# Two 32-byte tiles ahead of the products' operands

## The chip, the core and the metric

The kernel runs on one core of a Trainium2 chip. The core has a matrix engine (PE, with the loading of its stationary operand listed apart as PEld), a vector engine (DVE), a scalar engine (ACT), GpSimd (POOL) and a queue engine (SP) that starts the transfers. All engines share the on-chip memory SBUF, 128 partitions wide; the products are summed in PSUM. The metric is the device time of one execution in microseconds, lower being better.

## The reference

Two layers of a decoder over 512 tokens of width 1024. Each layer has two gated feed-forward blocks (FFN), a mixing block of three branches, and a gated input embedding; a norm stands before and after each.

```python
def swiglu(x, wg, wu, wd):
    return (jax.nn.silu(x @ wg) * (x @ wu)) @ wd
...
for i in range(DEPTH):
    f = swiglu(rmsnorm(h, g[0]), ffn_w_gate[i, 0], ffn_w_up[i, 0], ffn_w_down[i, 0])
    h = h + 0.5 * rmsnorm(f, g[1])
    z = rmsnorm(h, g[2]) @ w_in[i]
    ...                                   # spatial gating, RG-LRU, sparse attention -> y_a, y_b, y_c
    mix = jnp.concatenate([y_a, y_b, y_c], axis=-1) @ w_out[i]
    h = h + rmsnorm(mix, g[3])
    f = swiglu(rmsnorm(h, g[4]), ffn_w_gate[i, 1], ffn_w_up[i, 1], ffn_w_down[i, 1])
    h = h + 0.5 * rmsnorm(f, g[5])
    gate = jax.nn.sigmoid(rmsnorm(h, g[6]) @ ple_w_gate[i])
    h = h + rmsnorm(gate * (p[i] @ ple_w_proj[i]), g[7])
```

All of it is float32, and most of the work is in the products with the weights.

## The kernel before

The token axis lies along the free dimension: `h` is held as 8 blocks of 128 features by 512 tokens. Each float32 product is made of three products in the reduced type fp32r: both operands are split into a high part (rounded by ACT) and a low part (the rest, by DVE), and `mm3` (L271) adds high·high, high·low and low·high in one PSUM bank. In a name of the trace such as `mm<-xh,wh`, the first operand is the moving one (streamed, 256 or 512 columns) and the second the stationary one (loaded ahead, 128 columns).

Weights arrive as 4 KB per partition in a ring of eight `raw` tiles (L77, pool `p_raw`). ACT writes the high part into one of six `wh` tiles (L88) and DVE writes the low part into another `raw` tile; so `wh` is the high and `raw` the low stationary operand. Activations and everything else of 2 KB per partition lie in 56 slots tagged `big` and 7 tagged `scr` (L187): `xh`/`xl` (input of a block), `hh`/`hl` (hidden layer), `bh`/`bl` (combinations for the Strassen stage), `yh`/`yl` (branches' output), `zh`/`zl`.

An FFN runs as: 6 feature blocks of gate and up products; 16 more by Strassen's scheme (`strassen`, L725: seven products of 256 columns for each block, `bh`/`bl` moving, summed in `mm` and `o` banks); the down products (`hh`/`hl` moving, 512 columns; the last two blocks in halves of 256). The mixing block has the input projections, two stages in which the weights are the moving operand (`token_project`, L874: `wav` 256 columns and `wvg` 280 columns), the attention, and the `w_out` products (`yh`/`yl` moving). PE's order is written out by hand: each product depends on the one before it (L217).

Where a tile lies in SBUF is decided by the pools: `sb` lays one ring after another, in the order in which the tags are first asked for, each tile rounded up to a multiple of 32 bytes; `raw` follows behind it. `setup` (L278) asks for `ident`, `const`, `warm`, `h`, `cols`, and then come `big`, `scr`, `wh` and the small tags; `softplus` (L331) asks for some of the last small ones. So an odd number of 32-byte tiles ahead of a ring puts it at 32 bytes past a multiple of 64. In the built program:

| tile | first byte before | mod 64 | first byte after | mod 64 |
|---|---|---|---|---|
| `ident` | 16512 | 0 | 16512 | 0 |
| `h` | 17088 | 0 | 17120 | 32 |
| `cols` | 33472 | 0 | 33504 | 32 |
| `big` (first of 56) | 34144 | 32 | 34176 | 0 |
| `scr` (first of 7) | 148832 | 32 | 148864 | 0 |
| `wh` (first of 6) | 166304 | 32 | 166336 | 0 |
| `raw` (first of 8) | 196480 | 0 | 196544 | 0 |

The tiles of a ring are 1, 2 or 4 KB apart, so all of a ring have the same remainder. A `wvg` tile is the exception in use: it holds three pieces of 1120 bytes, so its middle piece lies 32 bytes off the other two.

Of the kernel before, what the change touches and what calls it, by code (L numbers as in the profile page):

```python
# [152 lines left out]
class Kern:  # L153
# [124 lines left out]
    def setup(self):  # L278
        nc, pool = self.nc, self.pool
        c = lambda name, shape: pool.tile(list(shape), F32, name=name)  # L280
        self.ident = c("ident", (128, 128))
        nc.gpsimd.memset(self.ident, 0.0)
        nc.gpsimd.affine_select(self.ident, self.ident, pattern=[[-1, 128]], compare_op=OP.not_equal,
                                fill=1.0, base=0, channel_multiplier=1)
        const = c("const", (128, 6))
        self.ones, self.mhalf, self.okrow = (const[:, i:j] for i, j in ((0, 1), (1, 2), (2, 6)))
        for t, value in ((self.ones, 1.0), (self.mhalf, -0.5), (self.okrow, 1.0)):
            nc.vector.memset(t, value)
        nc.gpsimd.affine_select(self.okrow[:, 0:1], self.okrow[:, 0:1], pattern=[[0, 1]],
                                compare_op=OP.is_ge, fill=0.0, base=-31, channel_multiplier=1)  # L290
        warm = self.small("warm", (128, 1), 1)
        nc.scalar.activation(warm, self.mhalf, AF.Silu)
        self.h = pool.tile([128, KD, S], F32, name="h")
        cols = c("cols", (128, L, 8 * KD + 20))
        nc.sync.dma_start(cols, self.dram["cols"])
        self.g = cols[:, :, :8 * KD].rearrange("p l (n k) -> p l n k", n=8)
        self.vec, at = {}, 8 * KD
        for name, n in (("conv_w", 8), ("conv_b", 2), ("ba", 2), ("bx", 2), ("lam", 2), ("cb1", 2), ("cb2", 2)):
            self.vec[name] = cols[:, :, at:at + n]
            at += n  # L300
        for n in (1, 5):
            nc.vector.tensor_scalar(self.g[:, :, n], self.g[:, :, n], 0.5, None, op0=OP.mult)
# [28 lines left out]
    def softplus(self):  # L331
        nc = self.nc
        lam = self.vec["lam"]
        sh = [128, L, 2]
        s = lambda n: self.small("sp" + n, sh, 1)
        e, u, u2, acc, m = s("e"), s("u"), s("v"), s("a"), s("m")
        self.pin("v", nc.vector.tensor_scalar(m, lam, -1.0, None, op0=OP.mult), False)
        nc.vector.tensor_max(e, m, lam)
        nc.scalar.activation(e, e, AF.Exp, scale=-1.0)
        nc.vector.tensor_scalar(u, e, 2.0, None, op0=OP.add)  # L340
        nc.vector.reciprocal(u, u)
        nc.vector.tensor_mul(u, u, e)
        nc.vector.tensor_mul(u2, u, u)
        terms = 9
        nc.vector.memset(acc, 1.0 / (2 * terms + 1))
        for i in range(terms - 1, -1, -1):
            nc.vector.tensor_mul(acc, acc, u2)
            nc.vector.tensor_scalar(acc, acc, 1.0 / (2 * i + 1), None, op0=OP.add)
        nc.vector.tensor_mul(acc, acc, u)
        nc.vector.tensor_scalar(m, m, 0.0, None, op0=OP.max)  # L350
        self.sp4 = self.small("sp4", sh, 1)
        nc.vector.scalar_tensor_tensor(self.sp4, acc, 2.0, m, op0=OP.mult, op1=OP.add)
        nc.vector.tensor_scalar(self.sp4, self.sp4, 4.0, None, op0=OP.mult)
        self.sp8 = self.small("sp8", sh, 1)
        nc.vector.tensor_scalar(self.sp8, self.sp4, -2.0, None, op0=OP.mult)
# [1104 lines left out]
```

## Time and profile before

| | |
|---|---|
| time, median of 3 runs | 2144.58 us (2143.4 to 2149.41) |
| the profiled execution | 2146.3 us, of which the span from first to last instruction is 2144.6 us |
| mean granted clock of PE | 0.993 of full speed |
| PE busy | 97% of the span, 14464 product records |
| PEld | 89% |
| DVE, ACT, POOL | 65%, 50%, 13% |
| HBM read | 192.78 MB, 92 GB/s over the span |

The page counts an engine as busy from the start of an instruction to its end, and products are pipelined: one is listed with 0.28 us while the next starts 0.12 us after it. So how fast PE goes is read from the starts of products that follow each other, not from their lengths. Where PE waits, the row says for whom.

### The profile page before, as it was taken

To read this page: it belongs to the slowest core of one execution; us is meant where nothing else is said; L and a number is where in the kernel's file an instruction comes from. 1 tells how busy PE (TensorE), PEld (TensorE's weight loads), DVE (VectorE), ACT (ScalarE), POOL (GpSimd) and SP (SyncE) were. 2 spreads that over 40 slices of the span, in tenths; PEclk is the share of its full clock that TensorE was granted. 3 is DMA by queue.
4 is the path that set the end of the run, shared out by engine and by line. 5 is a ranking of instruction groups with operands and counts; after the bars stand their busy time and mean duration, and the time that the engine had idled before them with its cause. 6 is when DMAs were issued, how large, how long until landed. Compare 5 with 4: busy or idle time off the path is not lost.

```text
span 2144.6 us, 36353 instructions
## 1 busy us (share of the span) xinstructions
PE 2082.0 (97%) x14464; PEld 1918.7 (89%) x14464; DVE 1389.1 (65%) x2505; ACT 1076.7 (50%) x2277; POOL 278.2 (13%) x392
## 2 busy tenths in 40 slices
PE   8989999999999999999999999999999999999997
PEld 8889978988999899879988998798889989998897
DVE  7877732757628888624688887246674488875264
ACT  4454532466735455533555555235676455555253
POOL 2000001311223000012330000021021410000133
PEclk9999999999999999999999999999999999999999
DMA  4243322432013233323222334224300232333221
GB/s 158 82 128 112 124 91 69 146 121 61 1 40 105 83 99 108 119 89 99 70 88 79 110 99 128 89 80 139 119 30 1 70 99 79 112 105 114 93 90 50
DMA packets 60706, 197.24 MB, mean 92 GB/s; under 512 B 6566, under 2 KB 10831, under 8 KB 60536
## 3 DMA queue, kind: packets, MB, share of 16 engines
q1 hardware_dynamic: 60536, 194.93, 28.9%
q8 instruction: 113, 1.85, 0.4%
q14 instruction: 57, 0.47, 0.1%
HBM read 192.78 MB, written 4.74 MB: 92 GB/s over the span
## 4 chain that ended last, share of the span: by engine, by line
PE 65%; DVE 19%; DMA 10%; ACT 4%; issue 2%; POOL 0%; SPq 0%; DVEq 0%; ACTq 0%; POOLq 0%
PE mm L211 51%; PE o L211 10%; DMA raw<-in_gu 9%; DVE raw L250 6%; DVE raw L93 4%; DVE xl L379 2%; PE t L215 2%; PE t L211 2%; DVE sz L93 1%; DVE h L537 1%; ACT wh L249 1%; DVE f L528 1%; DVE uv L791 1%; DMA raw<-in_dn 0%; ACT xh L374 0%
## 5 line engine op out<-in xcount | busy, mean ns | idle before, releaser
L250 DVE TENSOR_TENSOR raw<-raw,wh 128x512 fp32r<-128x512 f32 (+2 forms) x608 | 520.0, 881 | 370.2 <-ACT wh L249 359.0
L249 ACT ACTIVATE wh<-raw 128x512 fp32r<-128x512 f32 (+2 forms) x608 | 438.8, 763 | 395.9 <-DMA raw<-in_gu 128.6
L409 POOL TENSOR_TENSOR acc<-acc,sq 128x256 f32<-128x256 f32 x209 | 174.8, 846 | 1443.0 <-ACT sq L405 1438.4
L211 PE MATMUL mm<-xh,wh 128*128 128x256 f32 (+1 forms) x1088 | 351.2, 323 | 9.5 <-ACT wh L249 7.8
L211 PE MATMUL mm<-xl,wh 128*128 128x256 f32 (+1 forms) x1088 | 348.9, 321 | 9.0 <-DVE xl L379 8.6
L211 PE MATMUL mm<-xh,raw 128*128 128x256 f32 (+1 forms) x1088 | 348.6, 320 | 2.5 <-DVE raw L250 2.5
L211 PE MATMUL mm<-hh,raw 128*128 128x512 f32 (+1 forms) x880 | 310.3, 353 | 0.0
L211 PE MATMUL mm<-hh,wh 128*128 128x512 f32 (+1 forms) x880 | 310.0, 352 | 0.0
L211 PE MATMUL mm<-hl,wh 128*128 128x512 f32 (+1 forms) x880 | 308.6, 351 | 0.0
L211 PE MATMUL mm<-bh,wh 128*128 128x256 f32 x1024 | 289.0, 282 | 3.1 <-DVE uv L791 3.0
L211 PE MATMUL mm<-bh,raw 128*128 128x256 f32 x1024 | 287.9, 281 | 0.0
L211 PE MATMUL mm<-bl,wh 128*128 128x256 f32 x1024 | 287.3, 281 | 0.0
L211 PEld LDWEIGHTS mm<-xl,wh 128*128 128x128 f32 x1088 | 208.0, 191 | 28.0 <-DVE xl L379 12.5
L211 PEld LDWEIGHTS mm<-xh,wh 128*128 128x128 f32 x1088 | 208.5, 192 | 25.6 <-ACT wh L249 8.2
L211 PEld LDWEIGHTS mm<-xh,raw 128*128 128x128 f32 x1088 | 207.9, 191 | 19.1 <-DVE raw L250 3.6
L211 PEld LDWEIGHTS mm<-bh,wh 128*128 128x128 f32 x1024 | 192.9, 188 | 5.3 <-DVE uv L791 4.7
L211 PEld LDWEIGHTS mm<-bh,raw 128*128 128x128 f32 x1024 | 192.6, 188 | 0.0
L211 PEld LDWEIGHTS mm<-bl,wh 128*128 128x128 f32 x1024 | 192.6, 188 | 0.0
L211 PEld LDWEIGHTS mm<-hl,wh 128*128 128x128 f32 x880 | 165.5, 188 | 25.4
L211 PEld LDWEIGHTS mm<-hh,raw 128*128 128x128 f32 x880 | 165.0, 187 | 25.7
L93 DVE TENSOR_TENSOR raw<-raw 128x512 f32<-128x512 f32 x192 | 132.3, 689 | 86.0 <-DMA raw<-in_gu 84.0
L211 PEld LDWEIGHTS mm<-hh,wh 128*128 128x128 f32 x880 | 165.6, 188 | 24.5
(269 smaller groups left out, 4009.5 us busy)
## 6 DMA issues: line engine op xcount, KB each, us to landing
raw<-in_gu SPq DMA_DIRECT2D x176, 512.0 KB, 3.6
raw<-in_dn SPq DMA_DIRECT2D x88, 512.0 KB, 3.6
raw<-in_wi SPq DMA_DIRECT2D x28, 512.0 KB, 3.5
raw<-in_wo SPq DMA_DIRECT2D x16, 512.0 KB, 3.5
raw<-in_pg SPq DMA_DIRECT2D x16, 512.0 KB, 3.6
cw<-in_cw SPq DMA_DIRECT2D x16, 256.0 KB, 7.2
bias<-brow SPq DMA_DIRECT2D x16, 256.0 KB, 5.0
raw<-in_pp SPq DMA_DIRECT2D x6, 512.0 KB, 3.6
```

What stands on the lines that cost most here:

```text
L93: add = lambda o, a, b: k.pin("v", k.nc.vector.tensor_add(o, a, b))
L211: self.in_order(self.nc.tensor.matmul(out, lhs, rhs, start=start, stop=stop, skip_group_check=seeded), n if lhs.dtype == F32R and n >= 256 ...
L215: self.in_order(self.nc.tensor.transpose(out, src, self.ident), 256)
L249: for engine, ins in (("s", self.nc.scalar.activation(hi, src, AF.Copy)), ("v", self.nc.vector.tensor_sub(lo, src, hi.bitcast(F32)))):
L250: ("v", self.nc.vector.tensor_sub(lo, src, hi.bitcast(F32)))):
L379: return self.nc.vector.scalar_tensor_tensor(lo, self.h[:, k, a:b], self.g[:, l, n, k:k + 1], hi.bitcast(F32), op0=OP.mult, op1=OP.subtract)
L409: nc.gpsimd.tensor_add(acc[0], acc[0], q)
L528: self.pin("v", nc.vector.tensor_mul(f, f, bc2))
L537: self.pin("v", nc.vector.tensor_add(h, h, f))
L791: nc.vector.tensor_add(cur["uv"][:, right], cur["uv"][:, right], cur["c"])
```

## The change

Two tiles of 8 floats (32 bytes) are added, each with a memset on GpSimd so that it is used. `pad` comes behind `const` and shifts all that follows by 32 bytes; `padr` comes among the small tiles and shifts what follows it, the `raw` ring with it, by 32 bytes more.

```diff
@@ setup
         const = c("const", (128, 6))
+        nc.gpsimd.memset(c("pad", (128, 8)), 0.0)
         self.ones, self.mhalf, self.okrow = (const[:, i:j] for i, j in ((0, 1), (1, 2), (2, 6)))
@@ softplus
         nc.vector.tensor_scalar(m, m, 0.0, None, op0=OP.max)
+        nc.gpsimd.memset(self.small("padr", (128, 8), 1), 0.0)
         self.sp4 = self.small("sp4", sh, 1)
```

Of the 13,884 products of the program, 668 had the moving operand on a multiple of 64 bytes, 3,788 the stationary one, and 12 both. Afterwards it is 13,756, 13,832 and 13,704; left are the middle pieces of `wvg`, some products with a stride (`xx`), and the norm's columns (`r2c`, `rs`). Among the fp32r products (12,920 of the 13,884) none had both before.

No instruction changes place on PE, DVE, ACT or SP, and none gets another wait. On POOL two rows are added at the start of the program. Before, it stands there (the names are the tiles, `const` and `ident` being constants, `h` the input):

```order
L282 MEMSET ident 128x128
L283 ISA
L283 AFFINE_SELECT ident<-ident 128x128
L289 AFFINE_SELECT const<-const 128x1
L459 TENSOR_TENSOR acc<-h 128x256
```

And now, at the same place on POOL:

```order
L282 MEMSET ident 128x128
L286 MEMSET pad 128x8
L352 MEMSET padr 128x8
L283 ISA
L283 AFFINE_SELECT ident<-ident 128x128
L290 AFFINE_SELECT const<-const 128x1
L461 TENSOR_TENSOR acc<-h 128x256
```

Both memsets stand between the first memset and the first select, ahead of the first instruction that reads the input; the one written in `softplus` was moved up there by the scheduler.

## Rows read from the trace of the kernel before

**Rows 1.** the page's part 1: busy us (share of the span), instructions.

```profile
PE 2082.0 (97%) x14464; PEld 1918.7 (89%) x14464; DVE 1389.1 (65%) x2505; ACT 1076.7 (50%) x2277; POOL 278.2 (13%) x392
```

**Rows 2.** products by group: line, engine, tiles, shape xcount, busy us, mean ns, idle before.

```profile
L211 PE MATMUL mm<-bh,wh 128*128 128x256 f32 x1024 | 289.0, 282 | 3.1 <-DVE uv L791 3.0
...
L211 PE MATMUL mm<-hh,raw 128*128 128x512 f32 x528 | 210.9, 399 | 0.0
...
L211 PE MATMUL mm<-xl,wh 128*128 128x512 f32 x320 | 127.0, 397 | 0.0
...
L211 PE MATMUL mm<-yh,raw 128*128 128x256 f32 x160 | 45.0, 281 | 0.0
...
L211 PE MATMUL mm<-wh,xl 128*128 128x256 f32 x64 | 17.9, 280 | 0.0
L211 PE MATMUL mm<-raw,xh 128*128 128x256 f32 x64 | 17.9, 280 | 0.0
```

**Rows 3.** PE in order of time: start us, us, what; Strassen stage, layer 0.

```profile
199.80 0.28 PE L211 MATMUL mm<-bh,wh 128*128 128x256 f32 x1
...
211.93 0.28 PE L211 MATMUL mm<-bl,wh 128*128 128x256 f32 x1
```

**Rows 4.** PE in order of time, down halves of layer 0's first FFN, 256 wide.

```profile
373.77 0.28 PE L211 MATMUL mm<-hh,wh 128*128 128x256 f32 x1
...
385.89 0.28 PE L211 MATMUL mm<-xh,raw 128*128 128x256 f32 x1
```

**Rows 5.** PE in order of time, the same halves in layer 1.

```profile
1428.76 0.28 PE L211 MATMUL mm<-hh,raw 128*128 128x256 f32 x1
...
1440.89 0.28 PE L211 MATMUL mm<-xh,wh 128*128 128x256 f32 x1
```

**Rows 6.** PE in order of time, down stage of layer 0, 512 wide.

```profile
264.77 0.40 PE L211 MATMUL mm<-hl,wh 128*128 128x512 f32 x1
...
276.78 0.40 PE L211 MATMUL mm<-hl,wh 128*128 128x512 f32 x1
```

**Rows 7.** PE in order of time, w_out products of layer 0, 512 wide.

```profile
604.85 0.39 PE L211 MATMUL mm<-yh,raw 128*128 128x512 f32 x1
...
609.01 0.39 PE L211 MATMUL mm<-yh,raw 128*128 128x512 f32 x1
```

**Rows 8.** busy time by stretch: us, PE, PEld, DVE, ACT, POOL, PEclk, DMA.

```profile
149.50:153.30 3.80, 3.47 (x16) 3.47 (x17) 2.34 (x3) 2.52 (x7) 0.00 (x0) 0.50 0.49 138
640.00:740.00 100.00, 97.91 (x676) 90.12 (x675) 88.32 (x148) 55.18 (x110) 19.50 (x21) 1.00 0.28 90
```

**Rows 9.** PE in order of time, within the first stretch of rows 8.

```profile
150.21 0.42 PE L211 MATMUL o<-bl,wh 128*128 128x256 f32 x1
...
152.99 0.41 PE L211 MATMUL mm<-bh,raw 128*128 128x256 f32 x1
```

**Rows 10.** weight loads by group (PEld), columns as in rows 2.

```profile
L211 PEld LDWEIGHTS mm<-bh,raw 128*128 128x128 f32 x1024 | 192.6, 188 | 0.0
L211 PEld LDWEIGHTS mm<-bl,wh 128*128 128x128 f32 x1024 | 192.6, 188 | 0.0
```

**Rows 11.** PE in order of time, the wvg stage of layer 0.

```profile
469.79 0.29 PE L211 MATMUL mm<-wh,xh 128*128 128x280 f32 x1
...
471.35 0.29 PE L211 MATMUL mm<-wh,xh 128*128 128x280 f32 x1
...
472.90 0.29 PE L211 MATMUL mm<-wh,xh 128*128 128x280 f32 x1
```

**Rows 12.** ScalarE squares by group, columns as in rows 2.

```profile
L405 ACT ACTIVATE sq<-h 128x256 f32<-128x256 f32 x98 | 35.4, 404 | 1.2 <-DVE h L537 1.2
...
L405 ACT ACTIVATE sq<-f 128x256 f32<-128x256 f32 x14 | 5.6, 413 | 9.7 <-DVE f L861 6.9 <-DVE f L849 2.8
```

**Rows 13.** POOL in order of time, the kernel's start.

```profile
0.80 0.20 POOL L282 MEMSET ident<- 128x128 f32 x1 [0.29 <-POOLq L1452]
...
4.27 0.61 POOL L459 TENSOR_TENSOR acc<-h 128x256 f32<-128x256 f32 x1 [2.75 <-DMA h<-in_xT]
```

## Prediction

> **What bounds the kernel now.** I read the page's shares first. PE is busy 97% of the span, VectorE 65%, ScalarE 50% [rows 1], so the time is the number of products times the pace at which PE takes them, and little else. Next I read which products there are, by shape [rows 2]: 18 groups of 256-wide fp32r products (from `bh,wh` with 1024 down to `yh` with 160) hold 3×1024 + 3×768 + 1544 + 3×352 + 3×256 + 3×160 = 9,224, and six groups of 512-wide ones 3×528 + 3×320 = 2,544.
>
> Then the pace, from starts that follow each other without a wait. In the Strassen stage 103 steps take 211.93 − 199.80 = 12.13 us, 117.8 ns each [rows 3]. In the down halves of layer 0 it is 12.12 us for 101 steps, 120.0 ns [rows 4]; the same products in layer 1 take 12.13 us for 103 steps, 117.8 ns [rows 5]. So PE has two paces at one width, for the same work in the same form. The 512-wide products show two as well: 12.01 us for 51 steps is 235.5 ns in the down stage [rows 6], 4.16 us for 18 steps is 231.1 ns in the `w_out` products [rows 7]. [...]
>
> **The change part by part.** *The stationary operand.* `wh` goes from 32 past to a multiple of 64; `raw` was on a multiple already. So before has both kinds side by side, with the same moving tiles at 32: the load of `raw` takes 188 ns on average, that of `wh` 188 [rows 10], 1024 of each. Moving `wh` is worth 0.
>
> *The moving operand.* Almost all go from 32 to 0. Before has few at 0, all in the stages where the weights move. In `wav` the moving `raw` (at 0) and the moving `wh` (at 32) both last 280 ns, 64 of each [rows 2]. These lengths are no pace, so I also compare two steps of `wvg` with four triples each: from 469.79 to 471.35 the three moving pieces lie at 0, 32 and 0, from 471.35 to 472.90 at 32, 0 and 32, the stationary `xh`/`xl` at 32 throughout. They take 1.56 and 1.55 us for 12 steps of 280 columns, 130.0 and 129.2 ns [rows 11]. One more operand in three at a multiple of 64 thus made them 0.8 ns slower, if it did anything. Bounds for the pace of 256 columns: taken straight, the difference is 0.8 ns for a third of the products moved, 2.4 ns for all, 2.2 ns scaled to 256 columns; that is the way from 117.8 to 120.0. [...] I take 0, because both like-for-like comparisons lie nearest to it and the two steps of rows 11 differ by no more than the table's resolution (0.01 us).
>
> *What goes the other way.* `h` and `cols` move from 0 to 32 past. ScalarE's squares that read `h` (at 0) take 404 ns, those that read `f` (at 32) 413 [rows 12]. If the start made these 9 ns, the 98 squares of the group cost 98 × 9 ns = 0.9 us, most of it beside PE, and the 14 that read `f` win some back. VectorE's instructions on `h` lie in the same boundaries between blocks. I take 0 and keep 1 us.
>
> *The two memsets.* The 128×128 one takes 0.20 us, and a memset of 8 columns no more. They stand on POOL before the first instruction that reads the input, and that one waits 2.75 us for its transfer [rows 13]. So 0.4 us of 2.75: hidden. Without that cover the norm's sums, which PE needs much later, would start 0.4 us late.
>
> The sum, against the profiled execution: 2146.3 + 0 (stationary) + 0 (moving) + 0 (`h`) + 0 (memsets) = 2146.3 us. That execution lies 1.7 us above the median of the runs, so I expect a median of 2145 us.
>
> **The rivals.** [...]
>
> *PE falls into the faster of its two paces.* The same products at 117.8 and 120.0 in two layers say that the pace is a matter of how the reads fall in step, and new addresses may shift that. The Strassen stage, over half of the 9,224 (5,384 by its groups), runs at 117.8; of the rest a good part is at 120.0, and I estimate a third of all. All at 117.8 wins 9,224 / 3 × 2.2 = 7 us, all 512-wide ones at 231.1 win 2,544 × 4.4 = 11 us: 18 us, so 2127 us. Against it: nothing says in which direction a shift goes.
>
> *PE falls into the slower one.* The same mechanism with the other sign: the Strassen stage goes to 120.0 like the halves of rows 4. Then two thirds of 9,224 lose 2.2 ns, 13.5 us, and the 512-wide ones, already at the slower pace, nothing: 2159 us. For it speaks rows 11, where more operands on a multiple of 64 went with the slower pace. It decides from about half of these products on (6.4 us).
>
> *The change doesn't do what it says.* A few operands stay off, but nearly all fp32r products have both on; this one I drop.
>
> **How the numbers follow.** A measurement of this kernel can't tell less than about 0.3%, 6.4 us, from no change. No difference in pace: 0.53, 2145 us. Faster pace: 0.14, 2127. Both operands at once: 0.15, 1990, a good chance for a thing no row shows, because no row excludes it and it is the only way to the whole loss. Slower pace: 0.18, 2159. So faster 0.29, same 0.53, slower 0.18. The range reaches to the two paces with some us around them, 2103 to 2165, and leaves out the case of 1990 us and the edges, together about 2 in 10. The likeliest case alone lies within 2139 and 2151.
>
> **What the profile after would show.** If I am right, the Strassen stage keeps 117.8 ns a step and the down stage 235.5, and the loads of `wh` stay at 188 ns. [...] The squares of `h` going from 404 to about 413 while those of `f` go to 404 would show that ScalarE feels the start and that it doesn't matter for the time. What would make me wrong is a rule by which only products with both operands on a multiple of 64 are at their best, since no row here could show it.

## The result and the profile after

The changed kernel takes 2133.6 us (median of 4 runs, 2132.7 to 2136.9), the kernel before 2145.5 on the same chip: ratio 0.9946, 95% interval 0.9932 to 0.9961. It is 12 us faster; forecast was no change.

The page's part 1 of the changed kernel, as in [rows 1]:

```profile
PE 2061.1 (97%) x14464; PEld 1903.1 (89%) x14464; DVE 1388.4 (65%) x2505; ACT 1074.2 (50%) x2277; POOL 280.7 (13%) x394
```

PE is busy 20.9 us less (PEld, the loads of its weights, 15.6), the span 13.6 us shorter (2144.6 to 2131.0); the other engines run as many instructions as before, POOL two more, and their busy time moves by 2.5 us at most. So the products themselves go faster, and some of that is given back.

PE in order of time in the changed kernel, Strassen stage of layer 0, two of its stretches (start us, us, what):

```profile
201.84 0.28 PE L211 MATMUL o<-bh,wh 128*128 128x256 f32 x1
...
208.64 0.28 PE L211 MATMUL o<-bh,zh 128*128 128x256 f32 x1
...
231.00 0.28 PE L211 MATMUL mm<-bl,wh 128*128 128x256 f32 x1
...
242.90 0.28 PE L211 MATMUL mm<-bh,wh 128*128 128x256 f32 x1
```

A step is the time from the start of one product to the start of the next. 60 steps in 6.80 us are 113.3 ns each, 101 steps in 11.90 us are 117.8. Before had 117.8 in this stage [rows 3]; 113.3 is a pace that no row of before has.

The down halves of the first FFN and those of the second FFN, both in layer 0, again in order of time:

```profile
373.74 0.28 PE L211 MATMUL mm<-hh,wh 128*128 128x256 f32 x1
...
385.87 0.28 PE L211 MATMUL mm<-xl,wh 128*128 128x256 f32 x1
...
975.73 0.28 PE L211 MATMUL mm<-hh,raw 128*128 128x256 f32 x1
...
987.97 0.28 PE L211 MATMUL mm<-hh,raw 128*128 128x256 f32 x1
```

103 steps in 12.13 us: 117.8 where before had 120.0 [rows 4]. 108 steps in 12.24 us: 113.3. The 120.0 is gone.

Down stage of 512 columns, layer 0, and the `wvg` stage of 280 columns:

```profile
264.13 0.40 PE L211 MATMUL mm<-hl,wh 128*128 128x512 f32 x1
...
276.73 0.40 PE L211 MATMUL mm<-hl,wh 128*128 128x512 f32 x1
...
469.72 0.29 PE L211 MATMUL mm<-raw,xh 128*128 128x280 f32 x1
...
471.24 0.29 PE L211 MATMUL mm<-raw,xh 128*128 128x280 f32 x1
```

54 steps in 12.60 us are 233.3 ns (235.5 in [rows 6]); 12 steps in 1.52 us are 126.7 (130.0 and 129.2 in [rows 11]).

Over the whole trace I took every step that follows the one before it without a wait at full clock, and averaged 12 in a row. The shares of such dozens, and the mean step, which hangs to about 0.2 ns on which steps are counted:

| | 256 columns, before | after | 512 columns, before | after |
|---|---|---|---|---|
| paces (share) | 117.5 to 118.5 (67%), 119.5 to 120.5 (32%) | 113.3 (36%), 117.8 (56%) | 235.5 (87%), 231 (3%) | 233.3 (91%) |
| mean, ns | 118.6 | 116.2 | 235.2 | 233.4 |

PE's products stand in the same order in both traces, so the steps can be matched one by one. Those that are steady in both (no wait, one width, full clock) sum to −27.8 us: 256-wide products with a moving `x` 8.4 (2,233 steps), Strassen 6.8 (5,273), down halves 4.9 (1,040), `y` 2.4 (464), all of 512 columns 5.0 (2,646), the rest 0.4.

Where did the difference from 13.6 go? First the clock, and the steps that aren't steady. From the rows of the cores:

```profile
core 0: 2131.0 us, clock 0.990
```

Before it was 0.993 over its span. The stretches granted 0.50 add up to 43.0 us after and 34.0 before; a step of 256 columns takes 214 ns there [rows 9], so by estimate 9 us more of it cost about 9 × (1 − 117.8/214) = 4 us. Step by step, waits left out, the products that ran at 0.50 in one trace or both take 5.4 us more, and the steps at full clock that aren't steady (starts of stretches, changes of width) 1.5. That brings −27.8 to −20.9, which is what part 1 shows. Second, waits. PE's waits in the kernel before (who waits, for whom: us in total, times, longest):

```profile
PE mm L211 <- DVE xl L379: 8.6, 12, 2.2
PE mm L211 <- ACT wh L249: 7.8, 3, 6.6
...
PE mm L211 <- DVE uv L791: 3.0, 6, 1.1
```

and in the changed kernel, where the lines behind the edits have moved by one or two:

```profile
PE mm L211 <- DVE xl L381: 10.2, 13, 2.4
PE mm L211 <- ACT wh L249: 9.0, 3, 7.7
...
PE mm L211 <- DVE uv L793: 4.8, 6, 1.2
```

PE's idle time grew by 20.9 − 13.6 = 7.3 us, 4.6 of it in these three rows. As far as these rows show, PE arrives earlier at the same operands, and the engines that write them take as long as before to 1% (`xl` 696 ns against 690, `wh` 761 against 763, `uv` on DVE 415 against 414, in the mean).

What the change does beside the products is as small as the prediction had it. Weight loads and ScalarE's squares (columns as in [rows 10, 12]), and POOL's start (as in [rows 13]):

```profile
L211 PEld LDWEIGHTS mm<-bl,wh 128*128 128x128 f32 x1024 | 193.4, 189 | 0.0
L211 PEld LDWEIGHTS mm<-bh,raw 128*128 128x128 f32 x1024 | 192.8, 188 | 0.0
```

```profile
L407 ACT ACTIVATE sq<-h 128x256 f32<-128x256 f32 x98 | 35.5, 405 | 0.3
...
L407 ACT ACTIVATE sq<-f 128x256 f32<-128x256 f32 x14 | 5.6, 412 | 9.7 <-DVE f L863 6.8 <-DVE f L851 2.8
```

```profile
0.94 0.10 POOL L286 MEMSET pad<- 128x8 f32 x1
0.98 0.10 POOL L352 MEMSET padr<- 128x8 f32 x1
...
4.36 0.61 POOL L461 TENSOR_TENSOR acc<-h 128x256 f32<-128x256 f32 x1 [2.80 <-DMA h<-in_xT]
```

The squares of `h` keep their 405 ns at 32 past a multiple of 64, those of `f` their 412 at 0, so the 9 ns of [rows 12] go with the tile that is read and not with where it starts. The memsets take 0.1 us each and vanish in the 2.80 us wait.

### The profile page after: what moved, and what is told of

Same layout as the page of the kernel before. It is cut to its first block, busy times and chain, and to the rows that moved or that the text cites. A ratio compares the mean times of both kernels' runs of the same rounds, so it can differ in the third digit from the quotient of the medians.

```text
span 2131.0 us, 36355 instructions
## 1 busy us (share of the span) xinstructions
PE 2061.1 (97%) x14464; PEld 1903.1 (89%) x14464; DVE 1388.4 (65%) x2505; ACT 1074.2 (50%) x2277; POOL 280.7 (13%) x394
## 4 chain that ended last, share of the span: by engine, by line
PE 72%; DVE 15%; DMA 6%; ACT 4%; issue 2%; POOL 0%; DVEq 0%; SPq 0%; ACTq 0%; POOLq 0%
PE mm L211 55%; PE o L211 13%; DMA raw<-in_gu 6%; DVE raw L250 5%; DVE raw L93 2%; DVE xl L381 2%; PE t L215 2%; PE t L211 2%; DVE h L539 1%; ACT wh L249 1%; DVE sz L93 1%; DVE f L530 1%; DVE uv L793 0%; DMA raw<-in_dn 0%; ACT p L1320 0%
## 5 line engine op out<-in xcount | busy, mean ns | idle before, releaser
L211 PE MATMUL mm<-xh,wh 128*128 128x256 f32 (+1 forms) x1088 | 349.3, 321 | 11.7 <-ACT wh L249 9.0
```

What stands on the lines that cost most here:

```text
L211: self.in_order(self.nc.tensor.matmul(out, lhs, rhs, start=start, stop=stop, skip_group_check=seeded), n if lhs.dtype == F32R and n >= 256 ...
```

## The experiments

The theories, by the letters that the expectations use. A: new addresses only change how PE falls into step when a stretch starts, at random. B: products with both operands on multiples of 64 are faster. M and S: the start of the moving or of the stationary operand alone sets the pace (in the later runs S stands for another theory, which is told there). R: what counts is the offset between the moving and the stationary operand, the relative offset (start of the stationary one less start of the moving one), not where either of them lies. Later L: each relative offset has its own paces, one or two, and a stretch keeps the one that it starts in.

The offsets by kernel, in bytes past a multiple of 256: `wh` and `raw` against the moving tile. Before: 64 and 32, a mixture. After: 64 and 64. (`zl`, the low half of the second Strassen factor, lies among the moving tiles, at offset 0 in both.)

**One part alone.** Both keep the pad ahead of `raw`, and one more ahead of `wh` brings the stationary operands to the wanted place. The first kernel has the moving operands on multiples of 64 and the stationary ones at 32, the second the other way round.

```
@@ both: softplus(), ahead of sp4
+        nc.gpsimd.memset(self.small("padr", (128, 8), 1), 0.0)
@@ both: start(), ahead of the first wh
+        nc.gpsimd.memset(self.small("padw", (128, 8), 1), 0.0)
@@ the first only: setup(), behind const
+        nc.gpsimd.memset(c("pad", (128, 8)), 0.0)
```

> Moving operands (big, scr) on a multiple of 64 bytes, the stationary wh and raw both 32 past one. Theory M (the moving operand's start sets the pace): the whole gain of the change, about 2134 us, 113.6 to 117.8 ns a step in the layer-1 down halves as in the changed kernel. Theory S (the stationary operand's start): no gain, 2145 us, 117.8 to 120.0 ns. Theory B (both have to be on): no gain, 2145 us. Theory A (any new address can shift the pace): anything from 2127 to 2159.

> Stationary wh and raw on a multiple of 64 bytes, moving operands 32 past one. Theory M: 2145 us, paces 117.8 and 120.0 as before. Theory S: about 2134 us with 113.6 ns steps. Theory B: 2145 us. Theory A: anything from 2127 to 2159. The row of before that bears on it (raw on, wh off, 118 ns both) speaks for M or B.

Measured: 2142.6 us, ratio 0.9982 (0.9972 to 0.9992), and 2142.7, 0.9983 (0.9974 to 0.9992). Each is a little faster, and the two can't be told apart, in their paces either: 256 columns 117.86 and 117.84 ns, 512 columns 234.17 and 234.19. M and S, each of which had the whole gain for one kernel and nothing for the other, fall. What the two share is no alignment of either operand but the relative offset, 96 for both stationary kinds. That speaks for R. PE in order of time in the first kernel, Strassen stage, layer 0:

```profile
231.06 0.28 PE L211 MATMUL o<-bh,wh 128*128 128x256 f32 x1
...
242.93 0.28 PE L211 MATMUL mm<-bh,raw 128*128 128x256 f32 x1
```

101 steps in 11.87 us, 117.5 ns.

**A shift of 64 bytes**, the same pad with twice the size and no other:

```
+        nc.gpsimd.memset(c("pad", (128, 16)), 0.0)
```

> One pad of 64 bytes: all operands get new addresses, the remainders by 64 stay as in the kernel before (big, scr, wh at 32, raw at 0). Theories M, S and B: no gain, 2145 us, the same paces as before to 0.3 ns. Theory A: a change of over 6 us either way, and paces near 113.6 or 120 where before had others.

Measured: 2146.8 us, ratio 1.0003 (0.9992 to 1.0015), 256 columns 118.5 ns, 512 columns 234.9. Down stage of layer 0, as in [rows 6]:

```profile
264.82 0.40 PE L211 MATMUL mm<-hh,raw 128*128 128x512 f32 x1
...
276.82 0.40 PE L211 MATMUL mm<-hh,raw 128*128 128x512 f32 x1
```

51 steps in 12.00 us, 235.3 ns. The addresses of all these operands are new, the relative offsets are those of before, and so is the time. A isn't needed for any of the difference.

**`h` and `cols` at their old place**, the first pad behind them:

```
         nc.sync.dma_start(cols, self.dram["cols"])
+        nc.gpsimd.memset(c("pad", (128, 8)), 0.0)
```

> As the changed kernel, but the first pad stands behind h and cols, which thus stay on a multiple of 64 while all products' operands are on too. All theories on the products: the time of the changed kernel, 2134 us. If the shift of h to 32 past cost ScalarE and VectorE something on the path, it is up to 1 us faster, 2133 us, and the squares that read h take 404 ns instead of what the changed kernel shows.

Measured: 2133.0 us, 0.9935 (0.9920 to 0.9949), as the changed kernel. Where ScalarE's and VectorE's `h` lies costs nothing that can be measured here; the 1 us of the expectation is less than these intervals can tell.

**Nothing on a multiple of 64**: the pad ahead of `raw` alone, so that moving tiles, `wh` and `raw` all stay or come to 32 past one (left on one are the middle pieces of `wvg`). This is one half of the diff.

> Only padr: moving operands, wh and raw all lie 32 bytes past a multiple of 64; h stays on one. Theory B (both operands on a multiple of 64): no gain over moving alone or stationary alone, 2143 to 2147 us, 256-wide steps of 117.7 to 120 ns. Rival theory R (only the offset between moving and stationary operand counts, modulo 64, and it has to be the same for all products that follow each other): the whole gain of the change, 2134 us, with steps near 113.7 and 117.8 ns, because all offsets between them are 0, as in the changed kernel.

Measured: 2131.4 us, 0.9927 (0.9912 to 0.9943), the whole gain. PE in order of time, down stage of 512 columns, layer 0:

```profile
264.06 0.40 PE L211 MATMUL mm<-hh,raw 128*128 128x512 f32 x1
...
275.96 0.39 PE L211 MATMUL mm<-hh,raw 128*128 128x512 f32 x1
```

51 steps in 11.90 us, 233.3 ns, as after. 256 columns show 113.3 and 117.8 again, with 24% and 72% of the dozens where the changed kernel has 36% and 56%. B falls: the relative offsets are 64 and 64, as in the changed kernel, and hardly an operand is aligned.

**Products alone, by offset.** The layers are left out; groups of 24 products run on constant tiles with chosen starts.

> Leaves out the whole computation: it runs triples of products alone, 96 of 256 columns or 48 of 512 at each of 25 combinations of offsets (moving, first and second stationary tile, in bytes past a multiple of 64 with equal remainders by 1024), all twice, no transfers or other engines beside them. Theory B: 113 to 116 ns a step where moving and both stationary are multiples of 64 (0,0,0; 64,0,0; 64,64,64; 0,128,128), 117.5 to 120 at all others, 32,32,32 among them. Theory R: fast also at 32,32,32 and 16,16,16, slow at 0,32,32 and 32,0,0. Theory A (only the phase in which the reads fall in step, whatever the offset): the same combination gives different paces at its two places. If the start of an operand makes nothing without other engines beside, all are within 0.5 ns.

Measured: 256 columns 120.0 ns at relative offset 0 (also with both at 32 and both at 64), 118.3 at 16, 32 and 48, 117.8 at 64 and 192, 118.7 at 96 and 128, 116.7 at 224; 512 columns 226.7 at 0 and 16, 233.3 at 32, 64 and 224. Each of the two places of a configuration in the program gave the same pace. 256 gives what 0 gives (120.0), and the moving tile 128 ahead or 128 behind gives the same (118.7), which fits an offset that counts modulo 256. B and R both missed numbers: of these offsets 0 is the slowest for 256 columns and, with 16, the fastest for 512, and the 113.3 of the kernel didn't appear.

**How a stretch starts.** The same with four stretches for each 256-wide offset, three of them begun by one single product of another width:

```
+                if v:
+                    wid = (None, 320, 512, 128)[v]
+                    o = self.bank("o")
+                    self.mm(o[:, :wid], wh[:, sw:sw + 128], xh[:, m:m + wid], True, True)
```

> The kernel leaves the layers out and runs groups of 24 products alone, 256 or 512 columns wide, in the order of the kernel (high weights by high and low operand, low weights by high operand), at nine relative offsets between the stationary and the moving operands: 0, 32, 64, 96, 128, 160, 192 and 224 bytes past a multiple of 256, and the mixture of the kernel before (high weights 64, low weights 32). Each offset of the 256-wide products has four stretches of 48: one after a wait, the others behind one single product of 320, of 512 and of 128 columns, which shifts the step at which the stretch starts. Theory L (each offset has two paces, a stretch falls into one of them when it starts and keeps it): at offset 64 some of the four stretches go at 113.3 ns and some at 117.8, as the stretches of the changed kernel do (36% and 56% of its products); at the mixture 117.8 and 120.0; at 96 between 117.0 and 119.0. Rival O (each offset has one pace, and the 113.3 ns of the changed kernel need the traffic of its other engines): all four stretches of an offset agree within 0.5 ns, at 64 all go at 117.8. For 512 columns both expect 226.7 at offset 0 and 233.3 at 32, 64 and 224, and neither knows the others. The time itself should be about 300 us.

Measured at offset 64, the first and the second stretch in order of time:

```profile
96.02 0.28 PE L211 MATMUL mm<-pxh,pwr 128*128 128x256 f32 x1
...
100.44 0.28 PE L211 MATMUL mm<-pxh,pwr 128*128 128x256 f32 x1
...
101.62 0.28 PE L211 MATMUL mm<-pxh,pwr 128*128 128x256 f32 x1
...
106.33 0.28 PE L211 MATMUL mm<-pxh,pwh 128*128 128x256 f32 x1
```

39 steps in 4.42 us are 113.3 ns; behind one product of 320 columns 40 steps in 4.71 us are 117.8, and so to the end of the stretch. Behind 512 columns it is 113.3 again, behind 128 117.8. The same products at the same addresses on an otherwise idle core thus have the two paces of the changed kernel. O falls, L stands. (The map before this one began its stretches behind a wait too and had 117.8 at this offset both times, so a wait in front doesn't settle the pace.) For 512 columns the mixture of before shows its two:

```profile
473.68 0.40 PE L211 MATMUL mm<-pxh,pwh 128*128 128x512 f32 x1
...
483.62 0.39 PE L211 MATMUL mm<-pxl,pwh 128*128 128x512 f32 x1
...
484.92 0.39 PE L211 MATMUL mm<-pxh,pwh 128*128 128x512 f32 x1
...
494.80 0.40 PE L211 MATMUL mm<-pxh,pwh 128*128 128x512 f32 x1
```

43 steps in 9.94 us are 231.2 ns, 42 in 9.88 are 235.2: the `w_out` pace of [rows 7] and the down pace of [rows 6]. The whole map (last dozens of each stretch, ns):

| relative offset | 256 columns | 512 columns |
|---|---|---|
| 0 | 120.0 | 226.7 |
| 32 | 118.3 | 233.3 |
| 64 | 113.3 or 117.8 | 233.3 |
| 96 | 117.1 to 119.0 | 234.3 |
| 128 | 118.3 to 120.0 | 231.7 to 233.3 |
| 160 | 120.0 | 233.3 |
| 192 | 117.8 | 228.9 |
| 224 | 116.7 or 117.8 | 233.3 |
| `wh` 64, `raw` 32 (before) | 117.8 | 231.1 or 235.5 |

L missed one number: the mixture showed 117.8 in all four stretches, and not the 120.0 that a third of the kernel before has.

**Does the map hold in the kernel?** All at offset 0, by asking for the two small `r2c` tiles ahead of the moving ones:

```
         nc.sync.dma_start(cols, self.dram["cols"])
+        nc.gpsimd.memset(self.small("r2c", (128, 4), 2), 0.0)
...
+        nc.gpsimd.memset(self.small("padr", (128, 8), 1), 0.0)
```

> All moving and both kinds of stationary operands of the 256- and 512-wide products lie at one offset (relative offset 0; none on a multiple of 64 bytes), which no kernel so far had. Theory L (the relative offset sets which paces a stretch can have, as the runs of products alone gave them): the 256-wide products get slower than before, 120.0 ns in every stretch against 118.6 in the mean, which is 9270 x 1.4 = 13 us more; the 512-wide ones get faster, 226.7 against 235.2, which is 2520 x 8.5 = 21 us less; in sum 8 us less of pace, so 2133 to 2143 us, with the down products of 512 columns shorter and the Strassen stages longer than before. Rival S (what counts is that moving and stationary operands are in step at all, as in the changed kernel): paces as in the changed kernel (113.3 and 117.8; 233.4) and 2131 to 2136 us.

Measured: 2134.5 us, 0.9947 (0.9934 to 0.9960). Strassen stage and down stage of 512 columns, layer 0:

```profile
199.81 0.28 PE L211 MATMUL mm<-bl,wh 128*128 128x256 f32 x1
...
211.69 0.28 PE L211 MATMUL mm<-bl,wh 128*128 128x256 f32 x1
...
263.72 0.39 PE L211 MATMUL mm<-hl,wh 128*128 128x512 f32 x1
...
275.96 0.39 PE L211 MATMUL mm<-hl,wh 128*128 128x512 f32 x1
```

99 steps in 11.88 us are 120.0 ns, 54 in 12.24 are 226.7, both as L said from the products alone; over the trace 119.9 and 226.9. It reaches the time of the changed kernel in another way. Matched with before step by step, the steady 256-wide steps lose 12.9 us (10.3 of it in the Strassen stages) and the 512-wide ones win 21.8 (13.9 in the down stages), in sum −8.8 us with 0.1 elsewhere; L had said 13 more, 21 less and 8 less. The total can't tell L from S here; the paces can, and S had 113.3, 117.8 and 233.4. The span is 11.0 us shorter, and the 2.2 us that are left lie in waits and in steps that aren't steady.

**Each width at its own offset.** If L is right, 512-wide weights should lie at 0 and 256-wide ones at 64. That takes tiles 256 bytes longer, and room: 5 in place of 7 scratch buffers, with a kernel beside it that has the single pad (offset 64 throughout) and only this. The second stands on the pads of the kernel before, at offset 0; its shift of 16 numbers is 64 bytes.

```
@@ both
-        bufs = {"big": 56, "scr": 7}[tag]
+        bufs = {"big": 56, "scr": 5}[tag]
@@ two offsets (wh tiles and the Strassen factors likewise)
+            shift = 16 if self.narrow(name, c) else 0
-                    hi, lo = wh[:, cols], wl[:, cols]
+                    hi, lo = (t[:, shift + width * i:shift + width * i + width] for t in (wh, wl))
-        return self.kern.p_raw.tile([128, 1024], dt, tag="raw", name="raw")
+        return self.kern.p_raw.tile([128, 1088], dt, tag="raw", name="raw")
```

> The fifth kernel (one pad of 32 bytes ahead of the low weights, relative offset 64 for nearly all) with 5 in place of 7 scratch buffers of 2 KB; it is the kernel beside which the next one stands. Paces as in the fifth (113.3 and 117.8; 233.4). What the missing buffers cost no row shows: between 0 and 40 us, so 2131 to 2171.

> As the kernel with 5 scratch buffers, with tiles of weights 256 bytes longer, in which the weights of 512-wide products lie at relative offset 0 and those of 256-wide ones at 64 (the second Strassen factor of 512 products, and low weights of 256, at 0). Theory L: 512-wide 226.7 ns in place of 233.4, 2520 x 6.7 = 17 us less of pace, 256-wide 113.3 and 117.8 as before it but 120.0 for 768 of them, 2 to 4 us more; if waits take half of it back, as they did in the changed kernel, 6 to 8 us less than the kernel with 5 scratch buffers, if they take nothing 13 to 15 less. Rival S: 512-wide stays at 233.4 and the time within 3 us of it.

Measured: 2154.3 us (1.0040, 1.0025 to 1.0055) with 5 buffers, 2142.6 (0.9980, 0.9967 to 0.9993) with two offsets besides. The paces of 512 columns are 233.4 and 226.9, those of 256 columns the same 116.2 in the mean. So the offset of the 512-wide products gives 11.7 us of its 2520 × 6.6 = 17, and the missing buffers cost some 23 against the kernel with the single pad (2131.4), more than it.

**Cheaper room.** Two other ways to find it: 7 in place of 8 raw buffers, or one scratch buffer and one of two `zh` buffers.

```
@@ the first
-        self.p_raw = ctx.enter_context(tc.tile_pool(name="raw", bufs=8))
+        self.p_raw = ctx.enter_context(tc.tile_pool(name="raw", bufs=7))
@@ the second
-        bufs = {"big": 56, "scr": 7}[tag]
+        bufs = {"big": 56, "scr": 6}[tag]
-                h = k.pool.tile([128, 512], F32R, tag="zh", name="zh", bufs=2)
+                h = k.pool.tile([128, 512], F32R, tag="zh", name="zh", bufs=1)
```

> The two offsets of the kernel before this one (512-wide products at relative offset 0, 256-wide ones at 64), with all 7 scratch buffers again and with 7 in place of 8 buffers for raw weights, which makes the room. Theory L: paces as in that kernel (226.7; 113.3 and 117.8). Against 5 scratch buffers with one offset the two offsets gave 11.7 us, so from the fifth kernel's 2131 the time is 2120 if the missing raw buffer costs nothing, and later by what the weights then come too late: up to 30 us, no row shows it.

> The same two offsets with the room made by one scratch buffer (6 of 7) and one of the two buffers of the second Strassen factor's high part. Paces as in the kernel before it; 2120 us if neither is missed; the third of the Strassen pieces waits for the one buffer where it is read late, so 2120 to 2150.

Measured: 2179.2 us (1.0150, 1.0134 to 1.0167), 59 us above the 2120 where at most 30 were expected, and 2127.1 (0.9911, 0.9896 to 0.9925), within what was expected and the fastest of all. PE's waits, with 7 raw buffers:

```profile
PE o L221 <- ACT uv L802: 44.8, 53, 2.6
```

and with one `zh` buffer:

```profile
PE o L221 <- ACT uv L802: 7.9, 17, 1.2
```

In the second the pace of 512 columns is 226.8 ns (52 steps in 11.79 us below), that of 256 columns 117.0:

```profile
264.00 0.39 PE L221 MATMUL mm<-hh,raw 128*128 128x512 f32 x1
...
275.79 0.39 PE L221 MATMUL mm<-hh,wh 128*128 128x512 f32 x1
```

It lies below both given kernels; its interval and that of the one with the single pad (0.9912 to 0.9943) overlap at the edge.

## Why the prediction was wrong

It was wrong in the step on the moving operand ("I take 0"), together with the one on `wh` ("worth 0"), and in the way both were bounded. In place of these two zeros the runs showed 27.8 us less of pace, of which 13.6 reached the span of the profiled run and 11.8 the medians. Both steps of the prediction weighed each operand's own place, with comparisons in which one kind of operand differs and the other stays [rows 10, 11]. The runs show that no operand's own place counts: with everything at 32 the gain is whole (2131.4 us), and with one kind aligned and the other not it is a third of it, in time (4 us) and in matched steps (8.2 us), whichever kind is aligned. The quantity was the difference of two places, and before it wasn't one but two, 64 for `wh` and 32 for `raw`, in turns within each triple. The two stretches of [rows 11] differ in both offsets, 96 and 128 in the first, 0 and 32 in the second, so they were no test of one operand's place; the 280 columns went from 129.4 to 127.3 ns on average when each triple had one offset (192, 96 or 0 by piece). And equal loads of `wh` and `raw` [rows 10] say how long a load takes (188 ns), not how fast the products follow each other (117.8 or 120.0). That 2133.6 us lies within 2103 to 2165 is luck: the range was drawn around two other mechanisms, one on each side.

- *Both operands at once* (1990 us) falls: with nearly all products on multiples of 64 for both operands (2133.6 us) the kernel was no faster than with all at 32 (2131.4). The 1990 us, and the "whole loss" that its chance names, reckon with steps of about 107 ns for 256 columns and twice that for 512. By estimate that is half of the 214 ns that a step took where 0.50 of the clock was granted [rows 8, 9], 11 ns less than the 117.8 of before. No run shows such steps. In their place the runs showed a pace that hangs on the offset, and the least seen is 113.3 for 256 columns and 226.7 for 512, not together at any offset.
- *PE falls into the faster of its two paces* (2127 us) came nearest and had right that new addresses may bring other paces. That the reads fall in step was the author's guess; the runs show the paces (113.3 and 117.8 for the same products at the same addresses), not the reads. Its size rested on the two paces of before. What came was a new set: 117.8 for 120.0, 113.3 for a good third, 233.3 for 235.5. So 22.5 us of the 27.8 came from 256 columns (forecast 7) and 5.0 from 512 (forecast 11).
- *The slower pace* (2159 us): not seen. Its evidence, rows 11, showed the mixture and not the place.
- That the time is the products' pace "and little else" held for about half of the gain: 27.8 us of pace became 13.6 of span, by 5.4 us in products at the lower clock, 1.5 in steps that aren't steady, and 7.3 of waits.
- `h`, `cols` and the memsets: 0, as predicted, within what the kernel with `h` back can tell; the memsets by their 0.1 us within a wait of 2.80.

What stays open: why these offsets have these paces, what decides in which of its two a stretch starts, whether a kernel has the same shares of the two in every execution (there is one trace of each), and why the kernel before has a third of its 256-wide dozens near 120.0 where the mixture alone gave 117.8. That what runs just ahead of a stretch can decide was shown in products alone; that it can be steered in the kernel wasn't tried.

## What to carry to other kernels

Where PE is the bound (97% of the span here) and its products run behind each other, as the fp32r products of 256 and 512 columns do here, the distance between the moving and the stationary operand is worth a trial as a parameter of its own. Here, with one distance for all operands, it went with paces from 113.3 to 120.0 ns for 256 columns and from 226.7 to 234.3 for 512, and a distance of 256 bytes gave the 120.0 of distance 0. Try one distance for all operands of one stage (here 64 throughout took 2133.6 us, the mixture of before 2145.5) and choose it by width from a short map of products alone. The kernel followed that map to 0.3 ns where the map has one pace (120.0 and 226.7 at offset 0, 233.3 at 64); where it has two, their shares show only in the kernel, and the mixture of two distances wasn't followed. Aligning both to a round address did nothing by itself (2133.6 us with it, 2131.4 without). And when a pace shows two values for the same work, as 113.3 and 117.8 at offset 64, a comparison of steps says little until one knows which of the two each stretch was in.

## What was not expected of the hardware

- Of the offsets of the map, 0 is the slowest for 256 columns, together with 160 (120.0 ns), and the fastest for 512 (226.7); at 0 the kernel had the same (119.9 and 226.9).
- At offset 64 the same products at the same addresses ran at 113.3 or 117.8 ns; the stretch behind a wait had 113.3, the one behind one product of 320 columns 117.8 to its end.
- One pad of 32 bytes, which leaves hardly an operand on a multiple of 64, was worth 15 us of 2146.
